# A hybrid encoder step on one core: key transposes of two panels together, another staging place for one panel, weights asked for in four parts, one dependency fewer per value product

## The chip, the cores and the metric

The kernel runs on one core of a Trainium2 chip. The metric is the device time of one execution in microseconds, lower is better. Engine names are those of the profile: PE is the matmul engine (TensorE), ACT the ScalarE, DVE the VectorE, POOL the GpSimd, SP the engine that only issues DMAs here. Most DMAs stand in SP's queue, some in ACT's.

## The reference

One layer of a streaming encoder, for 1024 prompt rows and 64 sample rows (1088 together), in float32. What the changed code computes is the input projection and what is stored of it:

```python
xn = rms_norm(x, g_pre)
z = xn @ w_in                        # 1088 x 1024 times 1024 x 8208
xa, ga, q, k, v, gb, fl, ma, mb = jnp.split(z, np.cumsum(sizes)[:-1], axis=-1)
ua, conv_new = causal_conv(xa, conv_hist, conv_w, conv_b)
ya, h_new = rg_lru(ua, h0, ...)      # branch A
ya = ya * jax.nn.silu(ga)
logf = jax.nn.log_sigmoid(fl + b_f)
yb = fox_prompt(q, k, v, logf)       # branch B: softmax attention, 16 heads of 64
yb = yb.reshape(B, L, W_B) * jax.nn.silu(gb)
u = jnp.einsum('bsnw,nwd->bsnd', jnp.stack([ya, yb], axis=2), w_branch)
mix = jnp.sum(sigmoid(stack([ma, mb])) * u, axis=2) @ w_o
```

A residual sum, norms and a per-layer embedding follow. The keys k and the values v are outputs of their own, with one row per token (`k_prompt`, `v_prompt`, and `k_sample`, `v_sample` for the sample rows).

## The kernel before

**Numbers.** Every float32 factor is split into a high part and a rest (`wh`, `wl`; `xh`, `xl`): ACT copies the high part (`copy_act`, line 82), DVE subtracts it (`sub`, line 85), and PE makes three matmuls (high by high, rest by high, high by rest). Column blocks of 128 of the input projection are called panels. A panel's result has its 128 columns on the partitions and the 1088 tokens along the row.

**Stages of the span.** An opening (0 to 36 us) norms and turns x. Then come the value panels (to 129), two plain panels of a merge gate (`gate_panel`, 129 to 154, in three pieces each), twelve *quads* (154 to 448), attention (about 466 to 900) with the other plain panels mixed in, branch A (900 to 1100), the branch projections (to 1260), and the tail.

**Quads.** A quad is two panels made by a Strassen scheme: seven products of 24 matmuls each, in the order a11, s2, a12, s3, s1, a22, s4 (in the last quad s1 comes before a12), into three PSUM banks (`quad`, line 718). Between them stand p1 (ACT's copy of the first product), u2 = s2's product + p1 (DVE, line 802), u3 (DVE, line 813) and four results per quad, `put` (d1 half 0, d2 half 1, d2 half 0, d1 half 1). s3 adds into the bank of s2, so it can start only when u2 has been read out of it; a12 adds into a11's bank and waits in the same way for p1. a22 waits for u3. The eight first quads take turns: K (keys of two panels), Q (queries of two panels), K, Q and so on; the last four make other columns.

**What a key result passes through.** `put` writes it to a tile `ko` (DVE or ACT), ACT makes its high part `oh` and stores it, DVE makes the rest `kl` and SP stores it; both go to a scratch tensor for attention. The output `k_prompt` wants tokens on the partitions, so each `ko` is also turned by PE (`keys_out`: transposes into a PSUM tile `tpk`, lines 725 to 738), copied by ACT to an `st` or `kst` tile (there are two `st`, one `kst`) and stored by SP. These calls are put on a list, `owed`, and one is taken after each product. Query results use two tiles `qo`, key results two tiles `ko`. The `st` tiles are also what the plain panels are copied to before they are stored (`spill`, lines 279 to 282).

**Weights.** Panels' weights are loaded on SP, two panels (1 MB) or one (512 KB) in a DMA: in `look_ahead` (line 254) and, for the quads, in `load_pair` (line 552), where the load for quad i+2 is asked for when quad i starts. `split_pair` makes the sums s1, s2, s4 and the splits.

**Order.** Through the two plain panels and up to the first quad the order of ACT and DVE is that of the text (`tc.manual_schedule`). In the quads a scheduler puts the instructions of an engine in order; within a queue every engine goes strictly in order. Each DMA takes one of eight semaphores in turn, so a DMA is issued only when the one eight before it (SP's and ACT's counted together) has landed.

**Attention.** A value product (`values`, lines 1086 and 1087) takes the turned probabilities, a high part `th` that ACT copied out of PSUM and a rest `tl` that DVE made of both: `tl` first, then `th`.

Of the kernel before, what the change touches and what calls it, by code (L numbers as in the profile page):

```python
# [65 lines left out]
def hybrid_step(tc, a, o):  # L66
# [12 lines left out]
        return ap.bitcast(F32)  # L79

    def copy_act(out, in_, scale=1.0):
        act.activation(out=out, in_=in_, func=AF.Copy, scale=scale)  # L82

    def sub(eng, out, in0, in1):
        return eng.tensor_tensor(out=out, in0=in0, in1=in1, op=ALU.subtract)  # L85
# [147 lines left out]
    n_single = [0]  # L233
    ahead = deque()

    def look_ahead():

        while len(ahead) < 2:
            if held_back[0] and len(gates) <= n_gates - PLAIN // 2:
                return  # L240
            if not (gates or later):
                return
            src, tags = (gates or later)[0]
            if any(not e[3] and max(len(tags), e[4]) > 1 for e in ahead):
# [9 lines left out]
            tc.keep_in_program_order(sp.dma_start(dst, src.rearrange("(k p) n -> p k n", p=P)))  # L254
# [21 lines left out]
        look_ahead()  # L276
        return tag, w

    def spill(dst, t0, n, z):
        s = wpool.tile([P, GC], F32, name="st")  # L280
        copy_act(s[:, :n], z)
        act.dma_start(dst[:, t0:t0 + n], s[:, :n])

# [258 lines left out]
    TS = [tuple(tsum.tile([P, 4, HT], F32R, name=f"t{i}{c}")[:, :, :] for c in "hl") for i in (2, 3, 4)]  # L542
    T1, (T2, T3, T4) = blk(0, 1), TS

    def gate_panel(tag, w):
        return panel_steps(mm, *w, xs, lambda c, t0, n, z: spill(tag[1], t0, n, z))

    def load_pair(i):
        raw = sp_.tile([P, KT, 2 * P], F32, name="wraw", tag="wraw", bufs=1)[:, :, :] if i % 2 else raw_pair
        src = quads[i][0]  # L550
        for dst, s in zip([raw] if len(src) == 1 else panels(raw), src):
            sp.dma_start(dst, s.rearrange("(k p) n -> p k n", p=P))
        return panels(raw)

    def split_pair(i, raws_, got):
# [50 lines left out]
    pairs = [load_pair(0)]  # L606
    first_w = {}
    first_split = split_pair(0, pairs[0], first_w)
    steps = gate_panel(*plain_2)
    next(first_split)  # L610
    chunk(steps)
    next(first_split)
# [5 lines left out]
    r1.close()  # L618
    run(first_split)
    seq.__exit__(None, None, None)  # L620
    pairs.append(load_pair(1))
    kqp = sb("kqp")


# [94 lines left out]
                              start=(first and k == 0 and p == 0), stop=(k == 3 and p == 2),  # L719
                              skip_group_check=not first)  # L720

    def keys_out(p, s, c0, t0, n, blocks):

        cols = slice(p * P, (p + 1) * P)
        tp = mm.tile([P, 512], F32, name="tpk", tag="acc")
        for i in range(blocks):
            pe.transpose(tp[:n, i * P:(i + 1) * P], s[:, c0 + i * n:c0 + (i + 1) * n], ident[:, :])
        for i in range(0, blocks, 2):
            m = min(2, blocks - i)
            n_st[0] += 1  # L730
            st = (wpool.tile([P, GC], F32, name="st") if n_st[0] % 3 else
                  sp_.tile([P, 2 * P], F32, name="kst", tag="kst", bufs=1))
            copy_act(st[:n, :m * P], tp[:n, i * P:(i + m) * P])
            if t0 < SEQ:
                dst = o["k_prompt"][t0 + i * n:t0 + (i + m) * n, cols].rearrange("(b q) d -> q b d", q=n)
                sp.dma_start(dst, st[:n, :m * P].rearrange("p (b d) -> p b d", b=m))
            else:
                sp.dma_start(o["k_sample"][:, cols], st[:n, :P])

    def put(kind, arg, z, in1, h):  # L740

        tag = "ko" if kind == "k" else "qo"
        s = kqp.tile([P, HT], F32, name=tag, tag=tag, bufs=2)
        s3 = s.rearrange("p (c n) -> p c n", c=2)
        if in1 is None:
            copy_act(s3, z)
        else:
            dve.tensor_tensor(out=s3, in0=z, in1=in1, op=ALU.add)
# [12 lines left out]
        sp.dma_start(d[1, arg][:, h_], lo[:, :])  # L761
        if kind == "k":
            at = n_prod[0] + 3
            t0 = h * HT
            s = s[:, :]
            if h == 0:
                owed.append((at, lambda: keys_out(arg, s, 0, 0, P, 4)))
                owed.append((at, lambda: keys_out(arg, s, 4 * P, 4 * P, HT - 4 * P, 1)))
            else:
                owed.append((at, lambda: keys_out(arg, s, 0, t0, P, 3)))  # L770
                n = SEQ - HT
                owed.append((at, lambda: keys_out(arg, s, 3 * P, t0 + 3 * P, n - 3 * P, 1)))
                owed.append((at, lambda: keys_out(arg, s, n, SEQ, DEC, 1)))

    def seven(i, w, ahead_, last):
        B11, B21, B22 = blk(0, 0), blk(1, 0), blk(1, 1)
# [266 lines left out]
            spent(2 * (0.44 * w + 8))  # L1043
        return softmax(s, n, pr, mask[:, SEQ - n:])

    turned = {}
    n_diag = [0]

    def turn(u, g, q2, pr):
# [15 lines left out]
        at = book("A", now[0] + HOP_PE, per(A_HI, 512 - o0), lambda: copy_act(th[:, o0:], tp[:, o0:]))  # L1065
# [10 lines left out]
    def values(u, g, h, q2):  # L1076
# [2 lines left out]
            pvs[u] = pv_half()  # L1079
        pv = pvs[u]  # L1080
        th, tl = turned.pop((u, g))
        for j in range(2):
# [3 lines left out]
            pe.matmul(pv[:, :256], v, tl[:, c], start=(g == 0 and j == 0), stop=False)  # L1086
            pe.matmul(pv[:, :256], v, th[:, c], start=False, stop=(g == q2 and j == 1))  # L1087
        spent(480.0)
        if g < q2:
            return  # L1090
# [804 lines left out]
```

## Time and profile before

| what | before |
|---|---|
| three runs, us | 1521.35, 1520.63, 1514.87 (median 1520.63) |
| profiled execution, us | 1523.4, of which 1521.7 is the span |
| mean clock granted to PE in it | 0.985 of full |
| PE busy | 1459.8 us, 96% |
| DVE busy | 881.2 us, 58% |
| ACT busy | 687.9 us, 45% |
| POOL busy | 358.3 us, 24% |
| two plain panels, 130 to 154 us: PE busy | 22.91 of 24.00 us |
| quads, 153.9 to 448.2 us: PE busy, clock | 273.6 of 294.3 us, 0.97 |
| attention, 500 to 900 us: PE busy | 397.8 of 400 us |
| branch A, 900 to 1100 us: PE busy | 186.4 of 200 us |

A row of the timeline reads: start, duration, engine, line, operation, out<-in, form, count, and in brackets the idle time before it with what ended it. A row of the chain of waits has start, duration and the piece of work; one that begins with DMA is a transfer that something waited for. A row of the waits gives the engine and line that waited, what for, then total, times, longest. `SPq` and `ACTq` are the queues that issue DMAs. `p__1567`, `u__1895` and the like are p1 and u2 or u3 of one quad, with a buffer number. Matmuls overlap in the records, so a busy PE at a low clock looks as busy as one at full clock; the clock column tells them apart.

### The profile page before, as it was taken

The numbers are of one execution on the slowest core, as the hardware profiler recorded it, in microseconds if no ns is written. First come the engines' busy times: TensorE is split into PE (matmuls) and PEld (weight loads), VectorE is DVE, ScalarE is ACT, GpSimd is POOL, SyncE is SP. The second block draws the span as 40 slices with busy tenths as digits, with TensorE's granted clock in tenths as the row PEclk, the third lists the DMA queues.
The fourth block names the chain that finished last, engine by engine and source line by source line (L and its number), as shares of the span: only waits on it lengthen the run. The fifth ranks groups of instructions, "written<-read, shape, count | busy, mean of one in ns | idle before, by whom it ended". The sixth has DMA issues, their size and how long they took to land.

```text
span 1521.7 us, 26089 instructions
## 1 busy us (share of the span) xinstructions
PE 1459.8 (96%) x10096; PEld 1433.4 (94%) x10096; DVE 881.2 (58%) x1516; ACT 687.9 (45%) x1343; POOL 358.3 (24%) x443
## 2 busy tenths in 40 slices
PE   7999899998999999999999999989899999999998
PEld 7999899998998999999989989989899999999998
DVE  5464655454423666666556655999855544337644
ACT  4423334333213655666556545566544323334543
POOL 3011313231312323332333212555322000000001
PEclk8999999999999999999999999999999999999999
DMA  5365655654367566465556131111178534205111
GB/s 197 105 126 76 121 160 156 159 160 145 80 157 186 137 121 159 105 145 139 88 151 153 50 89 43 43 45 32 61 251 278 189 120 146 85 29 169 56 50 42
DMA packets 143575, 182.81 MB, mean 120 GB/s; under 512 B 21308, under 2 KB 114204, under 8 KB 143452
## 3 DMA queue, kind: packets, MB, share of 16 engines
q1 hardware_dynamic: 125788, 155.52, 39.6%
q10 hardware_dynamic: 17664, 25.64, 4.9%
q8 instruction: 79, 1.29, 0.3%
q14 instruction: 44, 0.36, 0.1%
HBM read 122.65 MB, written 58.46 MB: 119 GB/s over the span
## 4 chain that ended last, share of the span: by engine, by line
PE 74%; DVE 9%; DMA 7%; ACT 5%; issue 3%; POOL 2%; SPq 1%; ACTq 0%; DVEq 0%; POOLq 0%
PE quad L718 16%; PE acc L160 11%; PE acc L158 11%; PE acc L159 11%; PE tp L1062 4%; PE pv L1086 2%; PE pv L1087 2%; PE s L1040 2%; PE s L1041 2%; DMA d_ma<-st 2%; PE vacc L158 1%; PE vacc L159 1%; DMA out_k_prompt<-kst 1%; PE vacc L160 1%; DVE u L1330 1%
## 5 line engine op out<-in xcount | busy, mean ns | idle before, releaser
L160 PE MATMUL acc<-xh,wl 128*128 128x364 f32 (+1 forms) x768 | 253.2, 330 | 6.8 <-DVE wl L85 6.8
L158 PE MATMUL acc<-xh,wh 128*128 128x364 f32 (+1 forms) x768 | 253.9, 331 | 2.3 <-ACT st L82 2.3
L159 PE MATMUL acc<-xl,wh 128*128 128x364 f32 (+1 forms) x768 | 252.5, 329 | 0.0
L160 PEld LDWEIGHTS acc<-xh,wl 128*128 128x128 f32 x768 | 145.1, 189 | 7.4 <-DVE wl L85 7.4
L158 PEld LDWEIGHTS acc<-xh,wh 128*128 128x128 f32 x768 | 145.6, 190 | 3.6 <-ACT st L82 2.9
L159 PEld LDWEIGHTS acc<-xl,wh 128*128 128x128 f32 x768 | 145.3, 189 | 0.6
L85 DVE TENSOR_TENSOR wl<-w_raw,wh 128x1024 fp32r<-128x1024 f32 (+1 forms) x66 | 83.7, 1269 | 49.0 <-ACT wh L82 48.3
L1020 DVE CUSTOM_DVE_ANT_0 s<-s,mask 128x1024 f32<-128x1024 f32 (+7 forms) x128 | 95.5, 767 | 26.1 <-PE s L1041 25.7
L1025 POOL TENSOR_SCALAR pb<-pb,sm 128x896 f32<-128x896 f32 (+1 forms) x64 | 61.5, 962 | 202.6 <-DVE sm L1024 177.5
L718 PE MATMUL quad<-xh,wh 128*128 128x272 f32 x384 | 82.4, 296 | 6.4 <-ACT p__1567 L82 6.4
L82 ACT ACTIVATE wh<-w_raw 128x1024 fp32r<-128x1024 f32 (+1 forms) x66 | 64.3, 975 | 53.6 <-PE quad L718 20.6
L85 DVE TENSOR_TENSOR tl<-tp,th 128x512 fp32r<-128x512 f32 x96 | 65.7, 688 | 37.2 <-ACT th L82 37.2
L718 PE MATMUL quad<-xl,wh 128*128 128x272 f32 x384 | 80.1, 290 | 0.0
L718 PE MATMUL quad<-xh,wl 128*128 128x272 f32 x384 | 79.9, 290 | 0.0
L1022 ACT ACTIVATE pb<-s,nm 128x896 f32<-128x896 f32 (+1 forms) x64 | 61.1, 954 | 32.4 <-DVE nm L1020 26.7
L82 ACT ACTIVATE th<-tp 128x512 fp32r<-128x512 f32 x96 | 56.9, 596 | 41.4 <-PE tp L1062 37.1
L158 PE MATMUL acc<-wqh,hth 128*128 128x256 f32 x256 | 73.0, 285 | 0.0
L158 PE MATMUL acc<-wqh,mxh 128*128 128x256 f32 x256 | 72.5, 283 | 0.0
L159 PE MATMUL acc<-wql,mxh 128*128 128x256 f32 x256 | 72.4, 283 | 0.0
L160 PE MATMUL acc<-wqh,mxl 128*128 128x256 f32 x256 | 72.4, 283 | 0.0
L159 PE MATMUL acc<-wql,hth 128*128 128x256 f32 x256 | 72.4, 283 | 0.0
L160 PE MATMUL acc<-wqh,htl 128*128 128x256 f32 x256 | 72.4, 283 | 0.0
(535 smaller groups left out, 4282.3 us busy)
## 6 DMA issues: line engine op xcount, KB each, us to landing
w_raw<-in_w_in SPq DMA_DIRECT2D x15, 1024.0 KB
q<-d_q SPq DMA_DIRECT2D x48, 256.0 KB
k<-d_k SPq DMA_DIRECT2D x48, 256.0 KB
w_raw<-in_w_in SPq DMA_DIRECT2D x16, 512.0 KB
w_raw<-in_w_branch SPq DMA_DIRECT2D x8, 1024.0 KB
wraw<-in_w_in SPq DMA_DIRECT2D x5, 1024.0 KB
d_k<-oh ACTq DMA_DIRECT2D x16, 272.0 KB
d_k<-kl SPq DMA_DIRECT2D x16, 272.0 KB
```

The lines of the kernel that those rows point to most:

```text
L82: act.activation(out=out, in_=in_, func=AF.Copy, scale=scale)
L85: return eng.tensor_tensor(out=out, in0=in0, in1=in1, op=ALU.subtract)
L158: pe.matmul(out, ah, bh, start=start, stop=False)
L159: pe.matmul(out, ah, bl, start=False, stop=False)
L160: pe.matmul(out, al, bh, start=False, stop=stop)
L718: pe.matmul(acc[:, c, :CW], l[:, k, :], r[:, k, c * CW:(c + 1) * CW], start=(first and k == 0 and p == 0), stop=(k == 3 and p == 2), skip_ ...
L1020: at = book("D", now[0] + HOP_PE, per(D_MAX, n), lambda: dve.tensor_tensor_reduce(out=s[:, :n], in0=s[:, :n], in1=m, scale=-1.0, scalar=-N ...
L1022: free = book("A", at, per(A_EXP, n), lambda: act.activation(out=pr[:, :n], in_=s[:, :n], func=AF.Exp, scale=-1.0, bias=nm, accum_out=sm))
L1025: return free, book("G", at, per(G_NORM, n), lambda: pool.tensor_scalar(out=pr[:, :n], in0=pr[:, :n], scalar1=sm, scalar2=1.0, op0=ALU.mul ...
L1040: pe.matmul(s[:, c0:c0 + w], t["q1"][:, q0:q0 + P], t["k1"][:, c0:c0 + w], start=True, stop=False)
L1041: pe.matmul(s[:, c0:c0 + w], t["q2"][:HD + 4, q0:q0 + P], t["k2"][:HD + 4, c0:c0 + w], start=False, stop=True)
L1062: pe.transpose(tp[:, o0 + i * P:o0 + (i + 1) * P], pr[par][:, kb * P:(kb + 1) * P], ident[:, :])
```

## The change

Five edits:

1. `look_ahead` and `load_pair` ask for the same bytes in four DMAs of a quarter of the rows each (`load_panel`).
2. The second plain panel is copied to tiles of the quads' pool, `oh`, `oh` and `kl`, in place of `st`.
3. `load_pair(1)` stands earlier in the text.
4. `keys_out` turns the keys of two panels together, 128 by 256 to a copy and a store, once both panels are there; `ko`, `qo` and the results of the last four quads share one tag with four tiles; calls are due one product after they were listed, not three.
5. The `th` matmul of a value product is declared independent of ACT's copy of `th`.

```diff
     def copy_act(out, in_, scale=1.0):
-        act.activation(out=out, in_=in_, func=AF.Copy, scale=scale)
+        return act.activation(out=out, in_=in_, func=AF.Copy, scale=scale)
...
+    def load_panel(dst, src, pin=lambda inst: inst):
+
+        n = KT // 4
+        for i in range(4):
+            pin(sp.dma_start(dst[:, i * n:(i + 1) * n, :], src[i * n * P:(i + 1) * n * P].rearrange(
+                "(k p) n -> p k n", p=P)))
...
-            tc.keep_in_program_order(sp.dma_start(dst, src.rearrange("(k p) n -> p k n", p=P)))
+            load_panel(dst, src, tc.keep_in_program_order)
...
-    def spill(dst, t0, n, z):
-        s = wpool.tile([P, GC], F32, name="st")
+    def spill(dst, t0, n, z, s=None):
+        s = s or wpool.tile([P, GC], F32, name="st")
...
-    def gate_panel(tag, w):
-        return panel_steps(mm, *w, xs, lambda c, t0, n, z: spill(tag[1], t0, n, z))
+    def gate_panel(tag, w, room=lambda c: None):
+        return panel_steps(mm, *w, xs, lambda c, t0, n, z: spill(tag[1], t0, n, z, room(c)))
...
         for dst, s in zip([raw] if len(src) == 1 else panels(raw), src):
-            sp.dma_start(dst, s.rearrange("(k p) n -> p k n", p=P))
+            load_panel(dst, s)
...
-    steps = gate_panel(*plain_2)
+    pairs.append(load_pair(1))
+    steps = gate_panel(*plain_2, lambda c: f(sp_.tile([P, HT], F32R, name="oh", tag="oh", bufs=2)) if c < 2 else
+                       sp_.tile([P, HT], F32, name="kl", tag="kl", bufs=1))
...
-    pairs.append(load_pair(1))
...
-    def keys_out(p, s, c0, t0, n, blocks):
-
-        cols = slice(p * P, (p + 1) * P)
+    def keys_out(p, ss, c0, t0, blocks):
+
+        cols = slice(p * P, (p + 2) * P)
         tp = mm.tile([P, 512], F32, name="tpk", tag="acc")
-        for i in range(blocks):
-            pe.transpose(tp[:n, i * P:(i + 1) * P], s[:, c0 + i * n:c0 + (i + 1) * n], ident[:, :])
-        for i in range(0, blocks, 2):
-            m = min(2, blocks - i)
+        c = c0
+        for i, n in enumerate(blocks):
+            for j, s in enumerate(ss):
+                pe.transpose(tp[:n, (2 * i + j) * P:(2 * i + j + 1) * P], s[:, c:c + n], ident[:, :])
+            c += n
+        for i, n in enumerate(blocks):
...
-            copy_act(st[:n, :m * P], tp[:n, i * P:(i + m) * P])
...
+            copy_act(st[:n, :2 * P], tp[:n, 2 * i * P:2 * (i + 1) * P])
+            dst = o["k_prompt"][t0:t0 + n, cols] if t0 < SEQ else o["k_sample"][:, cols]
+            sp.dma_start(dst, st[:n, :2 * P])
+            t0 += n
...
-        tag = "ko" if kind == "k" else "qo"
-        s = kqp.tile([P, HT], F32, name=tag, tag=tag, bufs=2)
+        s = kqp.tile([P, HT], F32, name="ko", tag="ko", bufs=4)
...
-            at = n_prod[0] + 3
-            t0 = h * HT
-            s = s[:, :]
-            if h == 0:
-                owed.append((at, lambda: keys_out(arg, s, 0, 0, P, 4)))
...
+            kept[arg, h] = s
+            p = arg - arg % 2
+            if (p, h) in kept and (p + 1, h) in kept:
+                ss = [kept.pop((p + j, h)) for j in range(2)]
+                c = 0
+                for blocks in ((P, P), (P, P), (HT - 4 * P,)) if h == 0 else ((P, P), (P, SEQ - HT - 3 * P), (DEC,)):
+                    owed.append((n_prod[0] + 1, lambda c=c, blocks=blocks: keys_out(p, ss, c, h * HT + c, blocks)))
+                    c += sum(blocks)
...
+        def high():
+            turned_by[u, g] = copy_act(th[:, o0:], tp[:, o0:])
+
+        at = book("A", now[0] + HOP_PE, per(A_HI, 512 - o0), high)
...
+            tc.declare_no_dep(pe.matmul(pv[:, :256], v, th[:, c], start=False, stop=(g == q2 and j == 1)).ins, high.ins,
+                              reason="ordered through the low part")
```

Three places show how the instructions move. First ACT, around the second plain panel and the first quad's p1 (`p__`), before (`wh_1531` is the last weight split of the first quad, `DMAHW` a semaphore of a DMA):

```order
121 L82 ACTIVATE wh<-w_raw 128x1024
122 L82 ACTIVATE st<-acc 128x364 [waits DMAHW5_49,PE_49]
123 L282 DMA d_ma<-st 128x364 [waits DMAHW0_49,Activation_49]
126 L82 ACTIVATE st<-acc 128x360 [waits DMAHW6_49,PE_49]
127 L282 DMA d_ma<-st 128x360 [waits DMAHW1_49,Activation_49]
130 L82 ACTIVATE xh_108<-rb 128x2x544 x2
131 L82 ACTIVATE wh_1531<-s_1421 128x512 [waits Pool_49]
132 L82 ACTIVATE p__1567<-quad 128x544 [waits DVE_49,PE_49]
```

and with the change:

```order
121 L82 ACTIVATE wh<-w_raw 128x1024
122 L82 ACTIVATE oh<-acc 128x364 [waits PE_49]
123 L289 DMA d_ma<-oh 128x364 [waits Activation_49]
126 L82 ACTIVATE kl<-acc 128x360 [waits DVE_49,PE_49]
127 L289 DMA d_ma<-kl 128x360 [waits DMAHW4_49,Activation_49]
130 L82 ACTIVATE xh_108<-rb 128x2x544 x2
131 L82 ACTIVATE wh_1542<-s_1432 128x512 [waits Pool_49]
132 L82 ACTIVATE p__1579<-quad 128x544 [waits DVE_49,PE_49]
```

The order is the same; the copies of the panel no longer wait for a DMA, and the last store waits for one (a part of the quad's weights).

Second DVE, at u2 of the first Q quad (`u__1895` before, `u__1907` with the change), before:

```order
158 L748 TENSOR_TENSOR ko<-quad,u__1601 128x544 [waits PE_49]
159 L85 TENSOR_TENSOR wl<-w_raw,wh 128x1024 [waits DMAHW2_49,Activation_49]
160 L802 TENSOR_TENSOR u__1895<-quad,p__1856 128x544 [waits DVE_49]
161 L759 SCALAR_TENSOR_TENSOR kl<-ko,oh 128x544 [waits DMAHW6_49,Activation_49]
163 L813 TENSOR_TENSOR u__1973<-quad,p__1856 128x544 [waits PE_49]
```

and with the change:

```order
157 L757 TENSOR_TENSOR ko<-quad,u__1613 128x544 [waits PE_49]
159 L768 SCALAR_TENSOR_TENSOR kl<-ko,oh 128x544 [waits DMAHW7_49,Activation_49]
160 L808 TENSOR_TENSOR u__1907<-quad,p__1867 128x544 [waits PE_49,Activation_49]
161 L85 TENSOR_TENSOR wl<-w_raw,wh 128x1024 [waits DMAHW5_49,DMAHW3_49,DMAHW6_49,PE_49,Activation_49]
163 L819 TENSOR_TENSOR u__1991<-quad,p__1867 128x544 [waits PE_49]
```

u2 stands ahead of the weight split `wl` and no longer behind it; the last `ko` of the K quad before it waits for the product alone.

Third ACT, from the end of the first K quad to the Q quad's weight split (`tpk` are turned keys), before:

```order
147 L82 ACTIVATE wh_1815<-s_1571 128x512 [waits PE_49,Pool_49]
148 L82 ACTIVATE kst<-tpk 32x128 [waits PE_49]
151 L82 ACTIVATE p__1856<-quad 128x544 [waits PE_49]
152 L82 ACTIVATE st<-tpk 128x256 [waits DMAHW1_49,PE_49]
153 L82 ACTIVATE st<-tpk 128x128 [waits DMAHW2_49]
154 L82 ACTIVATE kst<-tpk 96x128 [waits DMAHW5_49,PE_49]
155 L82 ACTIVATE wh<-w_raw 128x1024 [waits PE_49]
```

and with the change:

```order
148 L82 ACTIVATE st<-tpk 128x256 [waits DMAHW2_49,PE_49]
149 L82 ACTIVATE st<-tpk 128x256 [waits DMAHW3_49]
152 L82 ACTIVATE p__1867<-quad 128x544 [waits PE_49]
153 L82 ACTIVATE kst<-tpk 128x256 [waits PE_49]
154 L82 ACTIVATE st<-tpk 128x256 [waits DMAHW1_49]
155 L82 ACTIVATE st<-tpk 32x256 [waits DMAHW3_49,PE_49]
156 L82 ACTIVATE wh<-w_raw 128x1024 [waits DMAHW6_49,PE_49]
157 L82 ACTIVATE kst<-tpk 128x256 [waits DMAHW7_49,PE_49,Activation_49]
158 L82 ACTIVATE st<-tpk 128x256 [waits DMAHW0_49,Activation_49]
```

The key copies come later, hold two panels each, and between p1 and the `wh` of the next quad two copies wait for a store instead of three.

More of the change, by code (lines that the diff above doesn't have):

```diff
@@ L732, in keys_out @@
                   sp_.tile([P, 2 * P], F32, name="kst", tag="kst", bufs=1))
-            copy_act(st[:n, :m * P], tp[:n, i * P:(i + m) * P])
[L734 to L738, printed above, removed]
+            copy_act(st[:n, :2 * P], tp[:n, 2 * i * P:2 * (i + 1) * P])
+            dst = o["k_prompt"][t0:t0 + n, cols] if t0 < SEQ else o["k_sample"][:, cols]
+            sp.dma_start(dst, st[:n, :2 * P])
+            t0 += n
+    kept = {}
     def put(kind, arg, z, in1, h):
-        tag = "ko" if kind == "k" else "qo"
-        s = kqp.tile([P, HT], F32, name=tag, tag=tag, bufs=2)
+        s = kqp.tile([P, HT], F32, name="ko", tag="ko", bufs=4)
         s3 = s.rearrange("p (c n) -> p c n", c=2)
@@ L1044, in scores @@
         return softmax(s, n, pr, mask[:, SEQ - n:])
-    turned = {}
+    turned, turned_by = {}, {}
     n_diag = [0]
@@ L1064, in turn @@
         turned[u, g] = (th, tl)
-        at = book("A", now[0] + HOP_PE, per(A_HI, 512 - o0), lambda: copy_act(th[:, o0:], tp[:, o0:]))
+        def high():
+            turned_by[u, g] = copy_act(th[:, o0:], tp[:, o0:])
+        at = book("A", now[0] + HOP_PE, per(A_HI, 512 - o0), high)
         return book("D", at, per(D_LO, 512 - o0), lambda: sub(dve, tl[:, o0:], tp[:, o0:], f(th[:, o0:])))
@@ L1081, in values @@
         th, tl = turned.pop((u, g))
+        high = turned_by.pop((u, g))
         for j in range(2):
@@ L1086, in values @@
             pe.matmul(pv[:, :256], v, tl[:, c], start=(g == 0 and j == 0), stop=False)
-            pe.matmul(pv[:, :256], v, th[:, c], start=False, stop=(g == q2 and j == 1))
+            tc.declare_no_dep(pe.matmul(pv[:, :256], v, th[:, c], start=False, stop=(g == q2 and j == 1)).ins, high.ins,
+                              reason="ordered through the low part")
         spent(480.0)
```

6 lines of the change are left out of this document (removed).

## The prediction

> **What bounds the kernel now.** I read the page first: how busy each engine is, and the chain that ended last.
>
> ```profile
> PE 1459.8 (96%) x10096; PEld 1433.4 (94%) x10096; DVE 881.2 (58%) x1516; ACT 687.9 (45%) x1343; POOL 358.3 (24%) x443
> PE 74%; DVE 9%; DMA 7%; ACT 5%; issue 3%; POOL 2%; SPq 1%; ACTq 0%; DVEq 0%; POOLq 0%
> ```
>
> TensorE is the bound: 1459.8 of a 1521.7 us span. Without removing matmuls there are only 61.9 us of its idle time to win, and what it loses at a low clock. So the second view is the list of TensorE's waits, and beside it ScalarE's waits on DMAs.
>
> ```profile
> PE quad L718 <- ACT p__1567 L82: 6.4, 1, 6.4
> PE quad L718 <- DVE u__3649 L802: 4.5, 1, 4.5
> PE quad L718 <- DVE u__2475 L802: 3.3, 1, 3.3
> PE quad L718 <- DVE u__1895 L802: 3.0, 1, 3.0
> PE quad L718 <- DVE u__3063 L802: 2.7, 1, 2.7
> PE s L1040 <- ACT pb L1022: 1.8, 1, 1.8
> PE s L1041 <- DMA q<-d_rows: 0.4, 1, 0.4
> ACT st L82 <- DMA d_ma<-st: 18.7, 3, 9.2
> ACT kst L82 <- DMA out_k_prompt<-kst: 12.1, 2, 6.8
> ```
>
> The first five rows make 19.9 us, all in the quads (154 to 448 us). I call the first stall A, the other four stalls B. The remaining 42 us stand in the opening, the branches and the tail, mostly behind VectorE, and nothing in the diff works there.
>
> Stall A in the chain of waits and on ScalarE's timeline:
>
> ```profile
> 146.77 0.37 SPq L552 DMA_DIRECT2D wraw<-in_w_in  x1
> 147.75 13.54 DMA d_ma<-st
> 161.38 0.47 ACT L82 ACTIVATE st<-acc 128x360 f32<-128x360 f32 x1 [9.24 <-DMA d_ma<-st]
> 165.82 0.60 ACT L82 ACTIVATE p__1567<-quad 128x544 f32<-128x544 f32 x1
> 166.48 0.82 PE L718 MATMUL quad<-xh,wh 128*128 128x272 f32 x2 [6.42 <-ACT p__1567 L82]
> ```
>
> A 1 MB weight load starts at 146.77; the plain panel's store of 147.75 takes 13.54 us to land; ScalarE cannot refill that `st` tile until 161.38 and stands 9.24 us. Everything behind it in its queue is late, last the copy p1, and TensorE's a12 product waits 6.42 us.
>
> Stall B, the first of four, on ScalarE, VectorE and TensorE:
>
> ```profile
> 184.78 8.76 DMA out_k_prompt<-kst
> 193.62 0.27 ACT kst L82
> 193.82 0.72 DVE L748 TENSOR_TENSOR ko<-quad,u__1601 128x544 f32<-128x544 f32 x1 [6.26 <-PE tpk L727]
> 194.87 1.23 DVE L85 TENSOR_TENSOR wl<-w_raw,wh 128x1024 fp32r<-128x1024 f32 x1 [0.32 <-ACT wh L82]
> 196.01 0.73 DVE u__1895 L802
> 196.78 4.80 PE quad L718 x24
> 202.02 3.01 PE quad L718 x24
> ```
>
> u2, which the s3 product needs, stands in VectorE's queue behind two things that are late: a `ko` that waits 6.26 us for key transposes to free its tile, and a `wl` whose `wh` stands on ScalarE behind the `kst` copy, itself waiting for an earlier key store (8.76 us to land). The last two rows show a second loss: 24 matmuls take 4.80 us after the stall and 3.01 us one product later. The windows say why, in their PEclk column (after five engines' busy times; then the DMA share and GB/s):
>
> ```profile
> 166.48:170.71 4.23, 4.23 (x18) 4.23 (x19) 4.23 (x3) 1.24 (x1) 3.53 (x3) 0.50 0.80 160
> 196.78:201.42 4.64, 4.64 (x25) 4.64 (x26) 1.36 (x2) 1.02 (x3) 0.00 (x0) 0.63 0.67 249
> 201.77:204.86 3.09, 3.09 (x27) 3.08 (x26) 1.77 (x3) 1.19 (x4) 0.00 (x0) 1.00 0.28 85
> ```
>
> The granted clock is 0.50 and 0.63 behind stalls A and B, and 1.00 elsewhere. Each stall is paid one and a half times.
>
> **The change, part by part.** *Second plain panel staged in oh, oh and kl.* Its three copies no longer take an `st` tile, so none waits for the store of 147.75. Two rows give the new times:
>
> ```profile
> 153.90 0.41 PE L718 MATMUL quad<-xh,wh 128*128 128x272 f32 x2
> 170.37 0.71 DVE L802 TENSOR_TENSOR u__1601<-quad,p__1567 128x544 f32<-128x544 f32 x1
> ```
>
> The plain panel's last piece ends where the quads begin, at 153.9, so its copy can start near 154.2 and not at 161.38: ScalarE and what follows it move up by 7.2 us. p1 then stands at 158.6 and ends before 159.9, where s2 ends and a12 wants to start. Removed: 6.42 us idle, and behind it the slow clock, 4.23 us at 0.50 where 2.1 would do, so 2.1 us. What is late next: u2, which ended at 171.1 behind the splits of the quad's inputs and weights on VectorE, ends at 163.9, and s3 could start at 162.9: 1.0 us. Net A: 6.4 + 2.1 − 1.0 = **7.5 us**, between 4 (if s3 inherits half the stall) and 8.5.
>
> *Keys of two panels together.* The transposes stay 80 on TensorE; copies and stores fall from 112 to 80 in all (14 to 10 per pair of panels), 1 KB rows in place of 512 B. What matters is order. On VectorE u2 now stands ahead of that `wl`, and no `ko` ahead of it waits for transposes, since the tag has four tiles and both panels are complete first. On ScalarE p1 stands ahead of the key copies that can wait for a store. So neither cause of B reaches s3. Idle removed: 3.0 + 3.3 + 2.7 + 4.5 = 13.5. Clock, from these four rows of the chain against 3.01:
>
> ```profile
> 247.63 4.57 PE quad L718 x24
> 296.87 4.82 PE quad L718 x24
> 348.05 4.81 PE quad L718 x24
> ```
>
> 1.79 + 1.56 + 1.81 + 1.80 = 7.0 us. Sum B: **20.5 us**, if no new wait takes its place. What is late next: the fourth and the last key copy each wait for a store issued about one product (3 us) earlier. If that lands as late as the 8.76 us above, ScalarE stands up to some 5 us, and behind it stand a `wh`, then on VectorE `wl` and u3, which the a22 product needs two products later, about 6 us of cover. So zero to little; without cover up to 5 − 3 = 2 us per quad, 8 in all, plus clock.
>
> *Weights in four parts.* The 44 loads become 176, 132 more issues on SP. One costs 0.4 us:
>
> ```profile
> L254 SPq DMA_DIRECT2D w_raw<-in_w_in x22: 368/446/1057, 90.2 to 1034.8; - x22
> SPq L930 <- PE s L1041: 32.8, 13, 5.0
> 750.65 0.44 SPq L930 DMA_DIRECT2D q<-d_q  x1
> 758.43 11.51 DMA q<-d_q
> ```
>
> 132 × 0.45 = 59 us of SP's time, spread over 1150 us of a queue that mostly waits. Behind a part in that queue stand key stores (quads) and the q and k loads of a head (attention). Those loads themselves wait for TensorE's scores (32.8 us, 13 times): the load at 747.93 is over 2.7 us before q is issued, 4 × 0.45 = 1.8 fits in. But the wait on the DMA eight issues back now often names a weight part, and at 758 a q load already lands late (11.51 us; TensorE idle 1.8 us, above). I put 2 us against the sum for such places; bounds 0 and 8. The gain: a store can slip in between two parts, which helps the key stores and is counted in B.
>
> [...]
>
> *One wait less per value product.* Groups on TensorE:
>
> ```profile
> L1086 PE MATMUL pv<-tl,vv 128*128 128x256 f32 x192 | 56.6, 317 | 0.4 <-ACT lo L82 0.4
> L1087 PE MATMUL pv<-th,vv 128*128 128x256 f32 x192 | 49.8, 282 | 0.0
> ```
>
> The `th` matmul has no idle time before it and is shorter than its neighbour. A satisfied wait costs nothing visible here: 0, at most some 5 us (the 35 ns between the two rows over 128 to 192 matmuls), which I don't take.
>
> *load_pair(1) earlier in the text* leaves SP's order as it is: 0.
>
> **Sum.** 7.5 + 20.5 − 2 = 26.0 us. The profiled execution took 1523.4 (span 1521.7 and 1.7 around it), 2.8 over the median of the runs, so it should come to 1497, and the median from 1520.6 to **1495**.
>
> **Rivals.** *R1, stall B only moves.* ScalarE still has three tiles for key copies and waits for a store three copies back; if they land in 9 or 10 us as now, `wh`, `wl` and u3 are late and a22 stalls in the Q quads. For it: the rows of 8.76 us, and ScalarE's 12.1 us. Against: fewer stores, quarter loads, two products of cover. Price: half of B comes back, 10 us, 1505; all of it, 1515. Chance 0.17 for both, a third of it the whole.
>
> *R2, the gain is given back downstream.* Attention would start earlier but wait for DMAs: the heads' loads near 449 us, where SP stands for d_ma stores. For it: the late q load at 758. Against: TensorE waits 0.4 us for the first head. Price: up to 15 us, 1509. Chance 0.07.
>
> *R3, slower: the quarter loads cost the heads their loads.* In the eight heads with a weight load ahead, q and k issue only when a part has landed; a 0.5 MB load at the 86 GB/s of this stretch takes 6.1 us:
>
> ```profile
> 148.00:159.00 11.00, 11.00 (x78) 11.00 (x77) 3.67 (x4) 2.69 (x4) 0.00 (x0) 1.00 1.01 86
> ```
>
> Eight times 6.1 plus 1.8 of slow clock is 63 us: 1495 + 63 = 1558 at worst. It decides once a head loses more than (26.0 + 7.6) / 8 = 4.2 us. Against: TensorE waits for no head's load now beyond 2.2 us in all, and before the change too the q load of several heads had to wait for the weight load as a whole. Chance 0.06. [...]
>
> *R4, the change hardly acts* (p1 or u2 late for another reason, gain under 7.6 us): chance 0.05, about 1517.
>
> **How the numbers follow.** The forecast has 0.65: 1488 to 1501 alone, from the 5 us of the value waits below and 7 us of unpriced waits above. 0.5% is 7.6 us, what a measurement tells from no change, so faster means under 1513.0. Faster: 0.65 + 0.11 (half of B kept) + 0.06 of R2 = 0.82 and a little of R1's rest, 0.84; within: the rest of R1 and R4, 0.10; slower: 0.06. The range for 8 in 10 goes from 1487 to 1510, down to where everything unknown helps, up to R1's half and R2.
>
> **What would show it.** In the changed profile: no `quad` wait on p1 over 1 us near 160, and no wait on u2 in the Q quads; clock 1.00 there; the stretch from the first quad to attention some 28 us shorter; attention and tail as long as before. It is wrong if `quad` waits for u3 or p1 by 2 us or more (R1), if `s` waits for q or k loads (R3), or if `pv` matmuls get shorter (the value wait was worth something).

## The result and the profile after

The changed kernel takes 1493.8 us (median of 4 runs, 1491.35 to 1494.94); the kernel before, on the same chip, takes 1519.74 (4 runs, 1514.87 to 1521.35). The ratio is 0.9832, 95% interval 0.9806 to 0.9859: 1.7% faster. The profiled execution took 1493.34 us, with a span of 1491.4.

The page of the changed kernel, busy times and the chain that ended last by engine:

```profile
PE 1451.8 (97%) x10096; PEld 1427.3 (96%) x10096; DVE 884.6 (59%) x1516; ACT 689.6 (46%) x1327; POOL 367.9 (25%) x443
PE 80%; DVE 8%; ACT 5%; DMA 3%; issue 2%; POOL 1%; SPq 0%; ACTq 0%; DVEq 0%; POOLq 0%
```

TensorE holds 80% of the chain where it held 74, and DMAs 3% where they held 7. The stretch of the quads, from the first quad matmul to the last, as windows of the two kernels (stretch, length, busy time and instructions of TensorE, its weight loads, VectorE, ScalarE and GpSimd, then granted clock, DMA share, GB/s); first before:

```profile
153.90:448.20 294.30, 273.61 (x2118) 271.37 (x2118) 151.53 (x224) 99.44 (x198) 79.96 (x73) 0.97 0.53 143
```

and after:

```profile
151.53:418.42 266.89, 265.19 (x2118) 263.86 (x2118) 154.35 (x224) 100.56 (x182) 83.13 (x73) 1.00 0.54 155
```

The same 2118 TensorE instructions take 27.4 us less. TensorE's idle time falls from 294.30 − 273.61 = 20.7 to 1.7 us, which is 19.0, and its busy time by 8.4 us, because the granted clock is 1.00 throughout. Around the quads the first one starts 2.4 us earlier, the way from the last quad to the first value product is 3.1 us shorter (35.4 to 32.3), and from there to the end it is 2.7 us longer (1038.0 to 1040.7). The four make −30.2 of the 30.3 us between the two spans. The medians are 25.9 us apart: the profiled execution of the kernel before, 1523.4 us, was 3.7 us above the median of its four.

TensorE's waits in the changed kernel, and ScalarE's on DMAs (total, times, longest):

```profile
PE s L1046 <- ACT pb L1028: 2.2, 1, 2.2
PE quad L726 <- DVE u__1613 L808: 0.9, 1, 0.9
PE quad L726 <- DVE u__4631 L819: 0.8, 1, 0.8
```

```profile
ACT st L82 <- DMA d_ma<-st: 7.9, 2, 4.3
ACT st L82 <- DMA out_k_prompt<-st: 7.5, 5, 3.1
ACT kst L82 <- DMA out_k_prompt<-kst: 5.5, 3, 2.3
```

None of the five stalls of before is left. The 0.9 us is s3 waiting for u2 behind the former stall A, the 0.8 us stood in before as well. ScalarE still waits for key stores, 3.1 us at most. The place of the first stall B, on ScalarE and VectorE in order of time (the last bracket is the idle time before, and what ended it):

```profile
177.40 0.62 ACT L82 ACTIVATE p__1867<-quad 128x544 f32<-128x544 f32 x1 [0.55 <-PE quad L726]
181.42 0.80 ACT L82 ACTIVATE st<-tpk 128x256 f32<-128x256 f32 x2 [3.12 <-DMA out_k_prompt<-st]
183.82 1.06 ACT L82 ACTIVATE wh<-w_raw 128x1024 fp32r<-128x1024 f32 x1 [1.60 <-PE quad L726]
...
180.91 0.72 DVE L808 TENSOR_TENSOR u__1907<-quad,p__1867 128x544 f32<-128x544 f32 x1 [0.71 <-PE quad L726]
184.91 1.22 DVE L85 TENSOR_TENSOR wl<-w_raw,wh 128x1024 fp32r<-128x1024 f32 x1 [3.27 <-ACT wh L82]
```

p1 stands ahead of the key copies and u2 ahead of `wl`, as the prediction had it. The key copy waits 3.12 us for a store, and nothing on TensorE feels it, as the chain shows:

```profile
161.57 12.35 PE quad L726 x96
173.92 0.44 PE tpk L737 x4
181.02 3.01 PE quad L726 x24
184.47 3.02 PE quad L726 x24
```

One row was not foreseen. On SyncE's queue the load of pair 1, which was issued at 146.77 before, is now issued at:

```profile
127.30 9.35 SPq L240 DMA_DIRECT2D wraw<-in_w_in  x4
```

### The profile page after: what moved, and what is told of

It reads as the page before. It is cut to its first block, busy times and chain, and to the rows that moved or that the text cites. A ratio compares the mean times of both kernels' runs of the same rounds, so it can differ in the third digit from the quotient of the medians.

```text
span 1491.4 us, 26313 instructions
## 1 busy us (share of the span) xinstructions
PE 1451.8 (97%) x10096; PEld 1427.3 (96%) x10096; DVE 884.6 (59%) x1516; ACT 689.6 (46%) x1327; POOL 367.9 (25%) x443
## 4 chain that ended last, share of the span: by engine, by line
PE 80%; DVE 8%; ACT 5%; DMA 3%; issue 2%; POOL 1%; SPq 0%; ACTq 0%; DVEq 0%; POOLq 0%
PE quad L726 16%; PE acc L160 13%; PE acc L158 13%; PE acc L159 13%; PE tp L1068 4%; PE pv L1096 3%; PE pv L1098 2%; PE s L1046 2%; PE s L1047 2%; PE vacc L158 1%; PE vacc L159 1%; PE vacc L160 1%; DVE u L1342 1%; DMA out_v_prompt<-v_sb 1%; PE vacc L456 1%
```

## The experiments

The theory in test was the prediction's: staging removes A; the new order of instructions removes B; parts, earlier text and the value wait are worth nothing or nearly so. Against it stood R1, by which the landing of the stores decides. The kernels ran in three groups, each on one chip with its own runs of the kernel before, whose medians were 1525.27, 1524.06 and 1527.10 us; so ratios are compared, and times only within a group. "Quads" is the length of the quads' stretch in the one profiled execution of each (before: 294.3); the ratio is of the medians, and the two can differ by some us. The changed kernel itself ran in none of these groups, so its 0.9832 isn't compared with the ratios here.

| kernel | median us | ratio and 95% interval | quads us |
|---|---|---|---|
| staging alone (plain_only) | 1518.79 | 0.9954, 0.9934 to 0.9974 | 293.1 |
| load_pair(1) earlier alone (move_only) | 1520.45 | 0.9962, 0.9940 to 0.9983 | 285.3 |
| one tag of four tiles alone (ko_shared) | 1515.94 | 0.9931, 0.9906 to 0.9956 | 290.1 |
| edit 4 alone (keys_only) | 1515.01 | 0.9926, 0.9901 to 0.9950 | 287.0 |
| four parts alone (parts_only) | 1507.33 | 0.9890, 0.9867 to 0.9913 | 284.7 |
| changed kernel without parts (no_parts) | 1511.95 | 0.9911, 0.9888 to 0.9935 | 281.7 |
| changed kernel without staging (no_plain) | 1492.48 | 0.9788, 0.9761 to 0.9814 | 266.6 |
| edit 4 and parts (keys_parts) | 1492.62 | 0.9791, 0.9764 to 0.9817 | 265.9 |
| one tag and parts (ko_parts) | 1493.29 | 0.9774, 0.9750 to 0.9798 | 266.0 |
| edit 4 and two parts (keys_parts2) | 1503.09 | 0.9848, 0.9824 to 0.9873 | 274.0 |
| edit 4 and eight parts (keys_parts8) | 1505.64 | 0.9858, 0.9834 to 0.9881 | 272.5 |
| changed kernel without edit 5 (no_wait) | 1494.69 | 0.9794, 0.9769 to 0.9818 | 266.9 |

### Stall A: staging, or the load's earlier start

plain_only is the kernel before with edit 2:

```diff
-    steps = gate_panel(*plain_2)
+    steps = gate_panel(*plain_2, lambda c: f(sp_.tile([P, HT], F32R, name="oh", tag="oh", bufs=2)) if c < 2 else
+                       sp_.tile([P, HT], F32, name="kl", tag="kl", bufs=1))
```

> Kernel before with one edit: the second plain panel is copied to oh, oh and kl in place of st. Theory of the prediction (the copies wait for an st tile, that is stall A): stall A falls to about 1 us, 7.5 us faster, ratio 0.995; the four stalls of the Q quads stay. Rival (the early load of the second quad's weights is what took stall A away, and the store is late whatever tile it comes from): under 2 us faster.

TensorE's waits in it:

```profile
PE quad L719 <- DVE u__1895 L803: 6.0, 1, 6.0
PE quad L719 <- DVE u__1689 L814: 1.8, 1, 1.8
```

and two links of its chain:

```profile
149.81 14.07 DMA wraw<-in_w_in
179.32 11.23 DMA out_k_prompt<-kst
```

The wait for p1 is gone, but in this execution the quads are only 1.2 us shorter. Two other things were late right behind it: the 1 MB load itself (14.07 us), whose weights a22 needs, for 1.8 us, and the key store of 179.32, which lands after 11.23 us and makes the first stall B 6.0 us instead of 3.0. TensorE came sooner to what it had to wait for anyway. The ratio, 0.9954, is nevertheless the expected 0.995, some 7 us less; where the executions that weren't profiled gained the rest, this trace doesn't show.

move_only is the kernel before with edit 3:

```diff
+    pairs.append(load_pair(1))
     steps = gate_panel(*plain_2)
...
-    pairs.append(load_pair(1))
```

> Kernel before with one edit: load_pair(1) stands ahead of the second plain panel in the text. Theory of the prediction: no change, SP's order is the same (ratio 1.000 within 0.002). Rival, from the trace after (the load was issued at 127.3 us there and at 146.8 before, because its tile lies in other memory): the load is over before the store of 147.75, the store lands in 2 to 3 us, stall A goes without any staging elsewhere: 7 to 8 us faster, ratio 0.995.

SyncE's timeline:

```profile
129.79 0.37 SPq L552 DMA_DIRECT2D wraw<-in_w_in  x1
```

and two of TensorE's waits:

```profile
PE acc L158 <- ACT st L82: 4.1, 3, 2.3
PE quad L718 <- DVE u__1601 L802: 0.5, 1, 0.5
```

The load starts 17 us earlier, before the stores instead of among them; no wait for p1 is left, s3 waits 0.5 us for u2 behind it, and the quads are 9.0 us shorter. Some of it is paid ahead: the first quad comes at 156.0 instead of 153.9, and plain panels wait 4.1 us for `st` where they waited 2.3. So this one line was worth as much in the quads as the prediction gave staging; in the ratio, 0.9962, it is some 6 us. What lets the load start earlier I infer and have not isolated: its place in SyncE's queue is the same, but the wait ahead of it names other work, so its tile must have other memory.

no_plain is the changed kernel with edit 2 taken back (the first diff, reversed):

> Kernel after with one edit undone: the second plain panel is copied to st again; load_pair(1) stays early. If the early load is what took stall A away: as the kernel after within 2 us. Theory of the prediction (the staging took it away): stall A is back, about 7.5 us slower than the kernel after.

TensorE has no wait for p1 in it either, and s3 waits 0.9 us for u2 as in the changed kernel. It takes 1492.48 us, against 1492.62 for keys_parts of the same group, which has neither staging nor the earlier load. Staging isn't needed once the rest is there.

### Stall B: order, or landing

ko_shared is the kernel before with one line of edit 4; keys are still turned panel by panel:

```diff
-        tag = "ko" if kind == "k" else "qo"
-        s = kqp.tile([P, HT], F32, name=tag, tag=tag, bufs=2)
+        tag = "ko"
+        s = kqp.tile([P, HT], F32, name=tag, tag=tag, bufs=4)
```

> Kernel before with one edit: ko and qo share one tag with four tiles; keys are still turned a panel at a time, 14 copies and stores per pair. Theory order (u2 comes late because of what stands ahead of it on VectorE; with the shared tag u2 stands ahead of the weight split again): all four stalls of the Q quads go, 18 to 20.5 us faster, ratio 0.987. Rival pairing (fewer and larger key stores are what frees the copies): the stalls stay in part, 0 to 8 us faster.

VectorE's timeline at the place of the first stall B:

```profile
198.07 0.73 DVE L759 SCALAR_TENSOR_TENSOR kl<-ko,oh 128x544 f32<-128x544 f32 x1 [12.09 <-DMA d_k<-kl]
198.71 0.72 DVE L802 TENSOR_TENSOR u__1895<-quad,p__1856 128x544 f32<-128x544 f32 x1
200.96 1.23 DVE L85 TENSOR_TENSOR wl<-w_raw,wh 128x1024 fp32r<-128x1024 f32 x1 [1.53 <-ACT wh L82]
```

The order is the wanted one: u2 stands ahead of that `wl`, and no `ko` waits for transposes there. But `kl`, ahead of u2, waits 12.09 us for the last store from its tile, and TensorE waits 6.6 us where it waited 3.0. Right order, and a store that lands late: the first stall is still there. The other three fall from 10.5 us together to 3.6 (0.5, 1.2 and 1.9), so order does act where the stores land earlier; B as a whole goes from 13.5 to 10.2 us.

keys_only is the kernel before with all of edit 4, whose diff stands above:

> Kernel before with one edit: keys of two panels turned and stored together, with the four shared tiles that this needs. Both theories: the four stalls of the Q quads go, 20.5 us faster, ratio 0.9865; stall A stays at 6.4 us.

```profile
PE quad L718 <- ACT p__1567 L82: 6.8, 1, 6.8
PE tpk L729 <- ACT st L82: 7.1, 3, 4.3
```

In these waits of TensorE A is unchanged. B has left u2 and sits in the key transposes, which wait for ScalarE to empty `tpk`, while ScalarE waits for key stores; at the transposes these waits are 8.2 us together, 1.1 of it for `kst`. The 20.5 us that the prediction gave to order came out as 7.3 us in the quads.

no_parts is the changed kernel with whole loads:

```diff
-            load_panel(dst, src, tc.keep_in_program_order)
+            tc.keep_in_program_order(sp.dma_start(dst, src.rearrange("(k p) n -> p k n", p=P)))
...
-            load_panel(dst, s)
+            sp.dma_start(dst, s.rearrange("(k p) n -> p k n", p=P))
```

> Kernel after with one edit undone: every weight load in one DMA again. Theory landing: the Q quads stall again on the key copies as with the paired keys alone (4.3, 1.8, 1.1 and 1.0 us at the key transposes, and the low clock behind them), 8 to 12 us slower than the kernel after, ratio to the kernel before 0.990. Theory order: as the kernel after within 2 us, ratio 0.983.

TensorE's wait:

```profile
PE tpk L730 <- ACT st L82: 10.6, 3, 6.7
```

and the row of ScalarE's timeline that causes the longest part of it:

```profile
196.77 0.64 ACT L82 ACTIVATE st<-tpk 128x256 f32<-128x256 f32 x2 [11.92 <-DMA out_k_prompt<-st]
```

The order is that of the changed kernel; the key copy now waits 11.92 us instead of 3.12. Of the whole gain less than half is left: 0.9911 against 0.9788 and 0.9791 for the two kernels with parts in the same group. This is R1's mechanism at work, at the transposes rather than at a22. Part of the loss lies ahead of the quads: the first one starts at 158.0 us here and at 152.9 in no_plain, and TensorE waits 3.3 us there for ScalarE's copies to `st`; what makes these late was not followed up.

### Parts alone, and why a store waits for a load

parts_only is the kernel before with edit 1:

```diff
+    def load_panel(dst, src, pin=lambda inst: inst):
+        n = KT // 4
+        for i in range(4):
+            pin(sp.dma_start(dst[:, i * n:(i + 1) * n, :], src[i * n * P:(i + 1) * n * P].rearrange(
+                "(k p) n -> p k n", p=P)))
```

> Kernel before with one edit: every weight load in four DMAs. Theory landing (a store of ScalarE's queue gets in between two parts but not into one load): the st copy before a12 waits 4 us less, stall A falls below 3 us and the two Q stalls that hang on a kst store (first and fourth) shrink by 2 us each; 6 to 12 us faster. Theory order (the prediction: A and B rest on order alone, and issues cost a little): between 2 us faster and 2 us slower.

The DMA queues while stall A's store was under way (packets, MB, share of 16 engines; q1 is SyncE's queue with the loads, q10 ScalarE's with the stores). Before, 148.5 to 158.5:

```profile
q1 hardware_dynamic: 854, 0.87, 101.8%
```

With parts, 146.5 to 155:

```profile
q1 hardware_dynamic: 747, 0.73, 95.9%
q10 hardware_dynamic: 144, 0.19, 5.9%
```

and the store in the chain:

```profile
145.90 9.30 DMA d_ma<-st
```

Before, not one packet of the store moved for ten microseconds while the load's 1 KB packets filled the engines (101.8%): its first one moved at 159.2, behind 957 of the load's 1024. With four parts (issued within 2.83 us in keys_parts) 144 store packets pass among the load's, and the store lands in 9.30 us instead of 13.54. Two of the stalls that this leaves, from TensorE's waits:

```profile
PE quad L725 <- DVE u__1910 L809: 2.7, 1, 2.7
PE quad L725 <- ACT p__1579 L82: 1.6, 1, 1.6
```

and the cause of the first on VectorE's timeline:

```profile
186.76 0.72 DVE L755 TENSOR_TENSOR ko<-quad,u__1613 128x544 f32<-128x544 f32 x1 [5.73 <-PE tpk L734]
187.50 1.23 DVE L85 TENSOR_TENSOR wl<-w_raw,wh 128x1024 fp32r<-128x1024 f32 x1
188.64 0.72 DVE L809 TENSOR_TENSOR u__1910<-quad,p__1871 128x544 f32<-128x544 f32 x1
```

A falls from 6.4 to 1.6 us. B stays, 2.7 to 3.2 us four times, and it is the order that keeps it: `ko` waits 5.73 us for transposes to free its tile, and u2 stands behind it and behind `wl`. Here the prediction's reading of B is right. The ratio, 0.9890, is a gain of some 17 us, above the 6 to 12 expected; the profiled execution is the slowest of its six and shows 11.5 of it.

### Both together

keys_parts is the kernel before with edits 4 and 1; ko_parts has only the shared tag and the parts, with keys turned panel by panel as before. Their diffs are those above.

> Kernel before with two edits: paired keys with four shared tiles, and loads in four DMAs. Theory landing: these two together take away the four Q stalls (20.5 us) and most of stall A, 22 to 27 us faster than the kernel before. Theory order: 20.5 us for B, stall A stays at 6.4 us.

> Kernel before with two edits: ko and qo share one tag with four tiles, loads in four DMAs; keys still turned a panel at a time. Theory order plus landing (u2 ahead of the weight split, stores landing in time; the pairing itself is not needed): the four Q stalls go, as paired keys with four parts within 3 us, ratio 0.980. Rival pairing (14 stores in place of 10 keep the three copy tiles busy): 4 to 8 us of waits at the key copies are left, ratio 0.985.

What is left of A in keys_parts, from TensorE's waits:

```profile
PE quad L725 <- ACT p__1579 L82: 0.5, 1, 0.5
```

and in ko_parts:

```profile
PE quad L725 <- ACT p__1579 L82: 0.7, 1, 0.7
PE quad L725 <- DVE u__4695 L820: 0.8, 1, 0.8
```

Both run as fast as the changed kernel less one edit in their own groups (no_plain 1492.48 us beside keys_parts, no_wait 1494.69 beside ko_parts), and in their profiled executions all stalls B are gone. In the quads of the profiled executions the shared tag alone takes off 4.2 us, the parts alone 9.6 and both 28.3, twice the sum. In the ratios they come nearer to adding up: 0.7% and 1.1% alone, 2.3% together. That one edit needs the other is therefore seen in the stalls of single executions, and in the medians only weakly. Turning keys in pairs, which gives the change its name, adds nothing that these runs can tell (0.9791 with it, 0.9774 without, in two groups, the intervals overlap), and neither do the 32 stores that it saves. Both kernels still issue pair 1 at 145 us and stage in `st`: with the parts, the store of A lands in 7.69 us in keys_parts and 8.40 in ko_parts, in time for p1.

### The number of parts

keys_parts2 and keys_parts8 differ from keys_parts in one number:

```diff
-        n = KT // 4
-        for i in range(4):
+        n = KT // 2
+        for i in range(2):
```

(and 8 for 4 in the other).

> Kernel before with paired keys, shared tiles and loads in two DMAs of 512 KB. Theory landing (a store gets its turn when the load DMA ahead of it ends, so its delay goes with the size of one DMA): the waits at the key transposes lie between the 8.2 us of the paired keys with whole loads and the none of four parts, 2 to 4 us; with the low clock 3 to 7 us slower than with four parts, ratio to the kernel before 0.982 to 0.985. Rival (any splitting will do): as with four parts within 2 us, ratio 0.979.

> Kernel before with paired keys, shared tiles and loads in eight DMAs of 128 KB. Theory landing: nothing is left to win, as with four parts within 2 us. Rival of the prediction (issues and waits eight DMAs back hold up the heads' loads): 176 more issues than with four parts, 79 us more of SP's time; q and k loads late and s waiting for them, 5 us or more slower than with four parts.

With two parts, a link of the chain:

```profile
144.76 13.38 DMA d_ma<-st
```

and TensorE's wait:

```profile
PE quad L725 <- ACT p__1571 L82: 6.2, 1, 6.2
```

A is back whole, while no stall B is. The time came out as expected for two parts, the place did not: it was to be lost at the key transposes. How much of the load goes ahead of the store can be counted. The packets of SyncE's queue from the load's first one until the store's first one moves, with two, four and eight parts (144.80 to 152.60, 146.39 to 151.70, 146.37 to 148.80; in these windows no packet of the store moves):

```profile
q1 hardware_dynamic: 683, 0.68, 99.2%
q1 hardware_dynamic: 467, 0.46, 98.3%
q1 hardware_dynamic: 216, 0.20, 97.2%
```

By my count the last of the store's data is through when about 1000, 590 and 330 of the load's 1024 packets are. So in these three runs the store got in not behind one part but behind about two: 1.3 to 2.0 halves, 1.8 to 2.3 quarters, 1.7 to 2.6 eighths. Two halves are the whole load, and both had been issued (143.78 to 144.70) before the store (144.76). Why it's two and not one, no run shows.

With eight parts the wait for p1 is 3.8 us, and there is a new one in attention. TensorE's wait there:

```profile
PE pv L1091 <- DVE diag0l L85: 4.2, 1, 4.2
```

and ScalarE's timeline at both places, with the store that the first one waits for (a link of the chain) at the end:

```profile
152.81 0.47 ACT L82 ACTIVATE st<-acc 128x360 f32<-128x360 f32 x1 [1.91 <-PE acc L160]
157.97 0.33 ACTq L289 DMA_DIRECT2D d_ma<-st  x1
158.34 0.63 ACT L82 ACTIVATE wh<-s 128x512 fp32r<-128x512 f32 x1 [5.06 <-DMA d_ma<-st]
...
523.59 0.33 ACTq L289 DMA_DIRECT2D d_ma<-st  x1
523.96 0.49 ACT L82 ACTIVATE diag0h<-tp 128x384 fp32r<-128x384 f32 x1 [5.48 <-DMA w_raw<-in_w_in]
...
149.31 8.27 DMA d_ma<-st
```

With eight parts ScalarE refills `st` at 152.81, 8.6 us sooner than before, without waiting for a store. What stops it is the issue of its next store, at 157.97, which waits for the store of 149.31, from another tile, to land; everything behind it in the queue is 5.06 us late. The same happens at 523.59, where the DMA waited for is one of the eight parts, 9.52 us under way. With eight parts there are more DMAs between two stores, and the wait of a new DMA for an older one, which the order of the eight semaphores asks for, held up ScalarE, which issues it, for 5.06 and 5.48 us. The two stalls are 8.0 of the 15.0 us between the profiled spans of eight parts and four; the rest wasn't followed up. With edit 4 and one, two, four and eight parts the ratios are 0.9926, 0.9848, 0.9791 and 0.9858: four is the best of those tried.

### The value wait

no_wait is the changed kernel without edit 5:

```diff
-            tc.declare_no_dep(pe.matmul(pv[:, :256], v, th[:, c], start=False, stop=(g == q2 and j == 1)).ins, high.ins,
-                              reason="ordered through the low part")
+            pe.matmul(pv[:, :256], v, th[:, c], start=False, stop=(g == q2 and j == 1))
```

> Kernel after with one edit undone: the th matmul waits for ScalarE's copy of th again. Theory of the prediction: no change within 2 us, mean of the th matmul 281 to 282 ns in both. Rival: up to 5 us slower than the kernel after, all of it between 450 and 862 us.

The group of the `th` matmuls in the changed kernel:

```profile
L1098 PE MATMUL pv<-th,vv 128*128 128x256 f32 x192 | 49.8, 281 | 0.0
```

In no_wait they take 282 ns each, and the span of the value products 412.95 us against 411.66. The time of no_wait comes from another group than the changed kernel's. Of the kernels in one group, keys_parts has the wait and no_plain hasn't (it has edit 3 besides): 1492.62 and 1492.48. Nothing can be seen of edit 5.

## Why the prediction was right, and where it was wrong

The time was predicted as 1495 and came out as 1493.8; the quads were to be some 28 us shorter and are 27.4. **What was right** is the account of what TensorE loses and what it gets back. Idle time: 6.4 + 13.5 − 1.0 = 18.9 predicted, 19.0 measured; in it s3's new wait for u2, 1.0 predicted and 0.9 measured. Clock: 2.1 + 7.0 = 9.1 predicted, 8.4 measured. The value wait: 0 predicted, and none seen.

**Which edit does it** was wrong in four steps.

*"Removed: 6.42 us idle" by staging.* Staging does take the wait for p1 away, and alone its ratio fits the 7.5 us. But in the profiled execution with whole loads 4.8 us came back within some 35 us, at a22 and at the first stall B, since the load and the key stores were late for TensorE anyway. In the changed kernel A is removed more than once, by the earlier load, by the parts and by staging, and staging adds nothing to the other two: the earlier load alone leaves no wait for p1, parts with edit 4 leave 0.5 us, parts alone 1.6.

*"load_pair(1) earlier leaves SP's order as it is: 0."* The order did stay. The term looked only at the queue and not at what the load's issue waits for; that changed, and the load moved by 17.0 us alone and by 19.5 in the changed kernel. Alone it takes 9.0 us off the quads.

*"So neither cause of B reaches s3", 20.5 us by order.* The causes were read rightly from the rows, but they are two, and the change of order removes one. With order alone (ko_shared, keys_only) the wait for stores goes to `kl` or to the transposes, and TensorE still loses 10.2 or 8.2 us to it; with landing alone (parts_only) `ko` and `wl` still stand ahead of u2, and 11.3 us are lost. The stalls go whole only with both, and the sum gave all of it to one. The two products of cover that the prediction put ahead of a late key copy didn't help in no_parts, where a store took 14 us, not the 8.76 us that the price was worked out from, and where the first to suffer were the transposes, through `tpk`, which the step hadn't in it.

*Parts: "I put 2 us against the sum", the gain "counted in B".* Undone, they cost 0.9911 − 0.9788 = 1.2% of 1524, 18 to 19 us (no_parts against no_plain, since the changed kernel isn't in that group); alone they give 1.1%. Outside the quads nothing was lost to them: the stretches before and behind gained 2.8 us together. That "a store can slip in between two parts" is what the four parts show: 144 of the store's packets pass among the load's, where the whole load let none through in ten microseconds. But it got in behind more than one part: 683, 467 and 216 of the load's packets were ahead of its first in two, four and eight parts, and with two it took 13.38 us.

**The rivals.** R1 was priced as a stall that stays with quarter loads, and it did not come, because the parts do what it needed; without them it is what is seen. R2 did not come: from the first value product to the end it is 2.7 us longer, less than two executions differ by. R3's mechanism, parts that hold up what is issued behind them, didn't show with four parts; with eight it did, at ScalarE's stores and not at the heads' loads, for 3.8 and 4.2 us of TensorE's time. Of the four sizes into which a 1 MB load was cut (with edit 4) 1 MB is the slowest and 256 KB the fastest, at ratios of 0.9926 and 0.9791. R4 did not come.

So the idle time and the clock were right because all five stalls went, and not for the reason given: the prediction needed landing to be good enough, and counted on order for it, while it booked the edit that makes the stores land as a loss. That 26.0 us predicted and 25.9 measured agree so closely is luck in part: between the two profiled executions it is 30.1 us, with no 2 us lost to the parts and 2.8 gained outside the quads.

## What to carry to other kernels

When a row says that an instruction is late behind two things, ask of each whether the edit removes it; here a change that removed one moved the wait to another tile in the queue (12.09 us to `kl`), and only undoing each edit and doing each alone showed which pair does the work. Read both the medians and the traces: one profiled execution can show less or more of a gain than the medians do (11.5 against some 17 us for the parts alone). Where small stores share the DMA engines with large loads, look at the queues' packets while a store is under way, and split the load until the stores land in time, but no further: with eight parts an issue on ScalarE waited 5.06 us for an older DMA. Halving it changed next to nothing for the store of stall A here (13.38 us, where it took 13.54). Of an earlier line in the text, check what the load's issue waits for, and not its place in the queue alone.

## What the runs showed of the hardware

In the kernel before, a store on one queue got no packet through for ten microseconds beside a 1 MB load on another, which held the engines at 101.8%; with the load in four parts 144 store packets got through and took 5.9%. Stores beside loads in two, four and eight parts did not improve in step: 13.38 us in two parts, 7.69 to 9.30 in four, and in eight the tile was free by 152.81 but the next issue stood until 157.97. In all three the store's first packets moved only behind 683, 467 and 216 packets of the load, 1.3, 1.8 and 1.7 parts. And the stall of 0.9 us in the changed kernel left the clock at 1.00 (161.57 to 173.92 us), where the four stalls B before, of 2.7 to 4.5 us, had cost another 1.6 to 1.8 us each (4.57 to 4.82 us for 24 matmuls against 3.01) and stall A, of 6.4 us, 2.1 by the prediction's estimate, at a granted clock of 0.63 and 0.50 behind the two that the windows show.
